# A hybrid state-space and delta-rule block: the modulation's shift leaves h and comes back as a bias per projection column

## The chip, the cores and the metric

The kernel runs on one NeuronCore of a Trainium2 chip. Its engines work side by side, each in the order of its own queue: TensorE (PE, matmuls; PEld is its loading of weights), VectorE (DVE), ScalarE (ACT), GpSimd (POOL), and SyncE (SP), which here only issues DMAs. SBUF is the working memory; PSUM holds what PE writes, in eight banks. The metric is the time of one execution in microseconds of device time, as the median of several runs.

## What is computed

The reference is one layer of an encoder block over 2048 tokens of 1024 features. The change touches its beginning only:

```python
mod = jax.nn.silu(c) @ ada_w + ada_b
shift, scale, gate = jnp.split(mod, 3, axis=-1)
h = rms_norm(x, norm_w) * (1.0 + scale[:, None, :]) + shift[:, None, :]
proj = h @ w_in            # 1024 x 3088
u_a, z_a, qkv, z_b, beta_fb, alpha_fb = jnp.split(proj, [o1, o2, o3, o4, o5], axis=-1)
...
y = jax.nn.gelu(y.reshape(bsz, seq, D_SSM)).astype(dt)          # S5 group, from u_a
qkv = jax.nn.silu(centred_depthwise_conv(qkv, conv_w))          # DeltaNet group
...
mix = jnp.concatenate([y_a, y_b], axis=-1) @ w_out
return x + gate[:, None, :] * mix                               # then a final rms_norm
```

There is one sequence, so shift, scale and gate are one vector of 1024 each. The projection of h is linear: what the shift adds to a column of `proj` is the same for all tokens, the product of the shift with that column of `w_in`.

## The kernel before

**Projection.** h is held transposed, features on partitions, as two f16 tensors `hhi` and `hlo` (a value and what its rounding leaves), 8 slices of 128 features by 2048 tokens. A block of 128 columns of `w_in` is held the same way, as `wh` and `wl`. One product (`gemm`, lines 244 to 247) is 24 matmuls of 128 by 512 tokens: for each of 8 slices wh by hhi, wh by hlo, wl by hhi, all into one PSUM bank. The 2048 tokens are four blocks of 512 (`NB`). `order` (line 182) lists 25 blocks of columns: 4 for u (the S5 input), then 3 z blocks, the 16 columns of beta and alpha (`ab`), and 17 further blocks of k, q, v and z.

**Scales.** Values are scaled by a power of two before they are rounded to f16, so that they fit. For weights, `w_max` takes a sum of squares on ACT (Square, line 203) and a ones-matmul on PE that spreads it over the partitions (line 208), and `w_cut` makes the scale on DVE (`pow2_root`), rounds `wh` on ACT (line 221) and makes `wl` on DVE (line 223). The inverse scale `iv` is multiplied by `ih`, the inverse scale of h (line 219). For h, `h_scale` takes a bound of the scale vector, and of the shift where there is one, over all features (a reduction on DVE and one on POOL).

**The opening stage** (lines 250 to 500) is written in the order in which each engine is to take its work (`manual_schedule`); every engine's queue follows the program's order. x arrives in blocks of 512 tokens; `x_square` (ACT), `x_root` and `x_scale` normalise it, `h_turn` transposes it on PE into PSUM, and `h_part` makes hhi and hlo. The modulation's columns are weighted sums of rows of `ada_w` (`aw_add` on DVE, the last two on POOL), summed over partitions by matmuls with a vector of ones (`mod_sum`, into the bank `pmod`). The scale's sum is made first, the shift's sum later.
- Block 0 is made twice. First without a shift and with a scale of its own, `s_0` (lines 377 to 380), so that the four products of u can run before the shift is known (lines 395 to 419, kept in four banks as `first`); at the end of the stage again with the final scale (lines 479 to 481).
- When the shift is known (lines 418 to 429), the final scale is set, `h_part` makes blocks 1 to 3 with the shift inside, in three steps: ACT writes scale times x plus shift in f32 (`hf`, line 318), POOL rounds it (line 320), DVE takes the difference (line 321).
- For block 0 of u alone, the shift comes as a bias: lines 435 to 439 multiply the u weights by the shift (one column, 24 matmuls a block of columns), and lines 453 and 454 empty the four kept banks with that bias. `u_out` (line 447) empties a bank with ACT and stores it to `u_d`.
- Then u of blocks 1 to 3, with `h_part` of the next block between the products. Beside them go loads and sums for the gate (`aw_add`, line 486), and in the last block `w_max` and `w_cut` of the first weights of the jobs (lines 495 to 500).

**The jobs** (`job`, line 984): for each of the other 21 blocks of columns, four products, each emptied by ACT into `raw` (line 1017, `conv_job`), `z` (line 1003, `z_job`) or `ab` (line 1116, `ab_job`); after the first product the next block's weights are loaded and squared, and later cut. After each product a `tick` (line 976) runs what is due of the convolutions, sums and transposes, and one step of the S5 group (`side`). PSUM has three tags: "gm" with two banks for products, "pt" with three and "sq" with three (line 85).

Of the kernel before, what the change touches and what calls it, by code (L numbers as in the profile page):

```python
# [23 lines left out]
KT = D // 128  # L24
# [16 lines left out]
def block(ctx, tc, x, c, ada_w, ada_b, norm_w, w_in, conv_w,  # L41
# [131 lines left out]
    ih = hpool.tile([128, 1], F32, name="ih")  # L173
    cw = s5t.tile([128, 12, 5], F32, name="cw")
# [20 lines left out]
    def w_max(i):  # L195
# [5 lines left out]
        m, ma, s, iv = [sp.tile([128, 1], F32, tag=f"w{j}", name=f"w{j}", bufs=6) for j in range(4)]  # L201
        wh, wl = [pools["wp", i < NU].tile([128, KT, order[i][1]], F16, tag=t, name=t) for t in ("wh", "wl")]
        A.activation(out=wl.bitcast(BF16), in_=ws, func=AF.Square, accum_out=m)
        wprep[i] = [None, ma, s, iv, wh, wl]
# [6 lines left out]
    def w_cut(i):  # L211

        if i >= len(order):
            return
        ps, ma, s, iv, wh, wl = wprep[i]
        ws = wraw[i]
        pow2_root(ps, ma, s, iv)
        if i >= NU:
            V.tensor_tensor(out=iv, in0=iv, in1=ih, op=ALU.mult)
        yield  # L220
        A.activation(out=wh, in_=ws, func=AF.Copy, scale=s)  # L221
        yield
        V.scalar_tensor_tensor(out=wl, in0=ws, scalar=s, in1=wh, op0=ALU.mult, op1=ALU.subtract)  # L223
        wprep[i] = (wh, wl, iv)
# [5 lines left out]
    def w_done(i):  # L230
        w = wprep[i][0:3]
        if i < NU:
            V.tensor_tensor(out=w[2], in0=w[2], in1=ih, op=ALU.mult)
        return w
# [15 lines left out]
    with ExitStack() as p0:  # L250
# [65 lines left out]
        def h_part(b, k, src):  # L316
            hf = hp.tile([128, 512], F32, tag="hf", name="hf", bufs=4)
            A.activation(out=hf, in_=src, func=AF.Identity, scale=aS[:, k:k + 1], bias=shS[:, k:k + 1])  # L318
            sl = slice(b * 512, (b + 1) * 512)
            P.tensor_scalar(out=hhi[:, k, sl], in0=hf, scalar1=1.0, scalar2=1.0, op0=ALU.mult, op1=ALU.mult)  # L320
            V.tensor_tensor(out=hlo[:, k, sl], in0=hf, in1=hhi[:, k, sl], op=ALU.subtract)
# [49 lines left out]
        s_0, ih0, s_h = [small(n) for n in ("s_0", "ih0", "s_h")]  # L371
        h_scale(bd, s_0, ih0, "h0")
        aS0, aS, shS = [small(n, KT) for n in ("aS0", "aS", "shS")]
        V.tensor_scalar(out=aS0, in0=aT, scalar1=s_0, scalar2=None, op0=ALU.mult)
        cuts = {i: w_cut(i) for i in range(1, NU)}

        for k in range(KT):
            A.activation(out=hhi[:, k, 0:512], in_=xk[:, k], func=AF.Copy, scale=aS0[:, k:k + 1])
            V.scalar_tensor_tensor(out=hlo[:, k, 0:512], in0=xk[:, k], scalar=aS0[:, k:k + 1], in1=hhi[:, k, 0:512],
                                   op0=ALU.mult, op1=ALU.subtract)  # L380
# [4 lines left out]
        ss = x_square(x1)  # L385
        first = []
        iv0 = small("iv0", NU)
# [7 lines left out]
        first.append(gemm(wprep[0], 0))  # L395
        next(cuts[2])
        next(cuts[2])
        shift_add(0, 1)
        whole(cuts[2])
        first.append(gemm(wprep[1], 0))  # L400
        whole(w_max(3))
# [3 lines left out]
        next(cuts[3])  # L405
        next(cuts[3])
        shift_add(2, 3)
        whole(cuts[3])
# [5 lines left out]
        first.append(gemm(wprep[2], 0, "sq"))  # L414
        turned = [h_turn(x1, k, t) for k, t in enumerate(("pt", "pt", "sq"))]
        first.append(bank("sq"))
        gemm_part(first[3], wprep[3], 0, range(4))
        mod_sum(0, [acc, aws[6]])
        gemm_part(first[3], wprep[3], 0, range(4, KT))
        xs_ = {2: x_load(2)}  # L420
        V.tensor_tensor(out=modc[:, 0:8], in0=pmod[:, 0:8], in1=adab[:, 0:8], op=ALU.add)
        V.scalar_tensor_tensor(out=bs_, in0=modc[:, 0:8], scalar=-1.0, in1=modc[:, 0:8], op0=ALU.mult, op1=ALU.max)
        V.tensor_tensor(out=bd, in0=bd, in1=bs_, op=ALU.add)
        h_scale(bd, s_h, ih, "h")
        V.tensor_scalar(out=aS, in0=aT, scalar1=s_h, scalar2=None, op0=ALU.mult)
        V.tensor_scalar(out=shS, in0=modc[:, 0:8], scalar1=s_h, scalar2=None, op0=ALU.mult)
        sh = [hp.tile([128, KT], F16, name=n, bufs=1) for n in ("shh", "shl")]
        V.tensor_copy(out=sh[0], in_=shS)
        V.tensor_tensor(out=sh[1], in0=shS, in1=sh[0], op=ALU.subtract)
        for k in range(3):  # L430
            h_part(1, k, turned[k])
# [1431 lines left out]
```

## Time and profile before

| | us |
|---|---|
| median of 3 runs | 1407.08 |
| lowest and highest | 1400.67, 1408.08 |
| the profiled execution | 1399.43 |
| its span, first to last instruction | 1397.7 |
| PE busy in the span | 1282.3 |
| DVE busy | 1017.6 |
| POOL busy | 708.1 |
| ACT busy | 672.5 |
| first u product starts | 40.18 |
| first product of block 1 starts | 85.74 |
| first product of the jobs starts | 165.82 |
| last z eviction of the jobs starts | 766.8 |

All rows but the first two come from one execution, taken by the hardware profiler. Times in its views count from the start of the span. A busy PE is modelled from the starts of its matmuls. The chain of waits goes back from the last instruction, at each step to what released it; the list of an engine's waits names the instruction that ended each wait last.

### The profile page before, as it was taken

What the parts mean: (1) busy time and instruction counts of PE and PEld (TensorE: products, weight loads), DVE (VectorE), ACT (ScalarE), POOL (GpSimd) and SP (SyncE); (2) the same over time, 40 slices, a digit from 0 to 9 for tenths busy, and PEclk for the clock granted to TensorE, in tenths of its full rate; (3) what the DMA queues carried; (4) which work ended last, traced back from release to release, by engine and by line L of the source; (5) the groups of instructions that cost most, each with busy time, mean ns of one, the idle gap of its engine ahead of it and who ended that gap; (6) DMA issues with size and microseconds to landing.
All of it is one profiled execution on the core that took longest, in us unless ns stands there. A gap on an engine that the chain in (4) does not pass through costs nothing.

```text
span 1397.7 us, 26524 instructions
## 1 busy us (share of the span) xinstructions
PE 1282.3 (92%) x9936; PEld 900.3 (64%) x9936; DVE 1017.6 (73%) x2095; ACT 672.5 (48%) x1348; POOL 708.1 (51%) x680
## 2 busy tenths in 40 slices
PE   2879897898999999999999699999999988998997
PEld 2445343355665555555554588999998877887885
DVE  4635579877765899998984667888878655865664
ACT  4445322444655454354445566776667423432332
POOL 3214223656540477878840766666553235654443
PEclk9789999999999999999999899999999999999998
DMA  9446343223457434343524533544335488686533
GB/s 308 173 86 187 92 87 87 64 82 89 121 163 191 132 106 129 99 143 95 156 80 135 163 83 96 175 144 143 115 132 184 150 294 279 223 312 211 181 107 112
DMA packets 255280, 206.43 MB, mean 148 GB/s; under 512 B 88496, under 2 KB 206256, under 8 KB 255152
## 3 DMA queue, kind: packets, MB, share of 16 engines
q1 hardware_dynamic: 255152, 204.75, 47.3%
q8 instruction: 78, 1.28, 0.4%
q14 instruction: 50, 0.41, 0.1%
HBM read 133.38 MB, written 73.33 MB: 148 GB/s over the span
## 4 chain that ended last, share of the span: by engine, by line
PE 67%; DVE 16%; DMA 4%; issue 3%; POOL 3%; ACT 2%; SPq 1%; DVEq 0%; POOLq 0%; ACTq 0%
PE gm L33 37%; PE sq L33 15%; PE pt L33 12%; DVE sq L1033 2%; DVE w L510 2%; DVE tm L510 1%; DVE xs L939 1%; PE pt L1077 1%; POOL w L510 1%; DMA y<-ya_d 1%; DVE t L510 1%; PE sq L1750 1%; DMA xt<-in_x_dram 0%; DVE r L1782 0%; DVE cv L1033 0%
## 5 line engine op out<-in xcount | busy, mean ns | idle before, releaser
L33 PE MATMUL gm<-hhi,wh 128*128 128x512 f16 (+1 forms) x784 | 294.4, 390 | 13.4 <-ACT wh L221 6.9
L33 PE MATMUL gm<-hhi,wl 128*128 128x512 f16 (+1 forms) x784 | 293.1, 388 | 8.2 <-DVE wl L223 8.2
L33 PE MATMUL gm<-hlo,wh 128*128 128x512 f16 (+1 forms) x784 | 293.4, 389 | 0.0
L33 PEld LDWEIGHTS <-wh 128*128 128x128 f16 (+1 forms) x1664 | 154.0, 100 | 199.7 <-issue 26.0
L33 PEld LDWEIGHTS <-wl 128*128 128x128 f16 (+1 forms) x832 | 79.8, 100 | 106.1 <-DVE wl L223 10.7
L1017 ACT ACTIVATE raw<-gm,w 128x512 f32<-128x512 f32 x48 | 33.1, 689 | 175.9 <-PE gm L33 175.9
L510 POOL TENSOR_TENSOR w<-w,w 128x512 f32<-128x512 f32 x32 | 50.2, 1578 | 87.9 <-DVE w L510 87.9
L33 PE MATMUL gm<-yh,gwh 128*128 128x256 f32 x256 | 80.0, 313 | 6.7 <-ACT yh L778 5.6
L1033 DVE SCALAR_TENSOR_TENSOR sq<-raw,cw,cv 128x512 f32<-128x512 f32 x48 | 55.2, 1151 | 29.6 <-ACT cv L1025 29.5
L1033 DVE SCALAR_TENSOR_TENSOR sq<-raw,cw,sq 128x512 f32<-128x512 f32 x96 | 72.6, 756 | 3.4
L33 PE MATMUL gm<-yl,gwh 128*128 128x256 f32 x256 | 73.3, 286 | 0.7 <-POOL yl L779 0.7
L1772 POOL TENSOR_TENSOR r<-r,xt 128x512 f32<-128x512 f32 x32 | 41.5, 1297 | 62.9 <-DVE r L1771 29.2
L33 PE MATMUL gm<-yh,gwl 128*128 128x256 f32 x256 | 72.5, 283 | 0.0
L1442 ACT ACTIVATE Y<-pt 128x512 f16<-128x512 f32 x96 | 58.0, 604 | 23.9 <-PE pt L33 23.2
L33 PE MATMUL sq<-S,kq 128*128 128x128 f32 x480 | 62.3, 281 | 0.0
L939 DVE TENSOR_TENSOR_SCAN xs<-c,w 128x255 f32<-128x255 f32 x64 | 61.1, 1013 | 1.1 <-POOL w L510 1.1
L33 PEld LDWEIGHTS sq<-S,kq 128*128 128x128 f32 x480 | 59.9, 196 | 2.0
L1421 DVE CAST_PREDICATED pb<-msk,pt 128x512 f16<-128x512 int8 x80 | 56.9, 714 | 5.5 <-PE pt L33 4.4
L1003 ACT ACTIVATE z<-gm,w 128x512 f32<-128x512 f32 x32 | 22.0, 688 | 80.0 <-PE gm L33 48.0
L33 PE MATMUL pt<-Y,nh 128*128 128x64 f16 (+1 forms) x896 | 56.3, 198 | 4.5 <-DVE Y L1429 4.2
L320 POOL TENSOR_SCALAR hhi<-hf 128x512 f16<-128x512 f32 x32 | 30.1, 960 | 54.9 <-ACT hf L318 47.9
L1443 ACT ACTIVATE YT<-pt 128x512 f16<-128x512 f32 x96 | 57.3, 597 | 0.0
(455 smaller groups left out, 3544.9 us busy)
## 6 DMA issues: line engine op xcount, KB each, us to landing
xt<-in_x_dram SPq DMA_DIRECT2D x25, 512.0 KB
ws<-in_w_in_dram SPq DMA_DIRECT2D x24, 512.0 KB
aw<-in_ada_w_dram SPq DMA_DIRECT2D x24, 512.0 KB
kq<-kT_d SPq DMA_DIRECT2D x32, 256.0 KB
kq<-qT_d SPq DMA_DIRECT2D x32, 256.0 KB
kt<-kt_d SPq DMA_DIRECT2D x32, 256.0 KB
vt<-vt_d SPq DMA_DIRECT2D x32, 256.0 KB
out_dram<-r SPq DMA_DIRECT2D x16, 512.0 KB
```

Of the source, the lines that this page charges most:

```text
L33: nc.tensor.matmul(out, lhsT, rhs, start=start, stop=stop)
L320: P.tensor_scalar(out=hhi[:, k, sl], in0=hf, scalar1=1.0, scalar2=1.0, op0=ALU.mult, op1=ALU.mult)
L510: (e or V).tensor_tensor(out=o, in0=a, in1=b, op=op)
L939: V.tensor_tensor_scan(out=o, data0=m1, data1=v, initial=0.0, op0=ALU.mult, op1=ALU.add)
L1003: A.activation(out=z, in_=ps, func=AF.Silu, scale=iv)
L1017: A.activation(out=raw[:, 2 + tb * 512:2 + (tb + 1) * 512], in_=ps, func=AF.Copy, scale=iv)
L1033: V.scalar_tensor_tensor(out=cv if j == 4 else ps, in0=raw[:, o + j:o + j + 512], scalar=cw[:, i12, j:j + 1], in1=cv if j == 1 else ps, op ...
L1077: nc.tensor.transpose(ps[:, j * 128:(j + 1) * 128], cv[:, j * 128:(j + 1) * 128], ident)
L1421: V.copy_predicated(out=cols(PB[d][li], b, d), mask=mb, data=pp.rearrange("p t (n b) -> p t n b", b=b))
L1442: A.activation(out=cols(Y[d], b, d), in_=pa.rearrange("p t (n b) -> p t n b", b=b), func=AF.Copy)
L1443: A.activation(out=cols(YT[d], b, 1 - d), in_=pb.rearrange("p t (n b) -> p t n b", b=b), func=AF.Copy)
L1772: P.tensor_tensor(out=r[:, ns], in0=r[:, ns], in1=xt[:, ns], op=ALU.add)
```

## The change

The shift is taken out of h and is added behind each product, as a bias per column.
- `h_part` has no shift and two steps: ACT rounds scale times x to `hhi`, DVE makes `hlo` from the same source, the PSUM bank. POOL has no part in it. It serves block 0 too, which is made once, with one scale of h (`s_h`, `ih`) that is known before the shift.
- The shift gets a scale of its own (`s_s`, inverse `ish`) and stays in SBUF as two f16 columns per slice, `sh`.
- A new function `w_bias` multiplies one block of weights by the shift: 24 matmuls of one column into a "pt" bank, and a copy on ACT with the scale `ib`, which is the weights' inverse scale times `ish` (one more multiplication on DVE for each block of weights). It is called for the four u blocks in the opening stage, and at the start of every job ahead of its first product; for the beta and alpha columns it runs 96 matmuls, since their weights stand at four places.
- Evictions of the products take the bias with them (Identity and Silu with a bias in place of Copy and Silu).
- In the opening stage the u products of block 0 and the first two of block 1 are emptied without a bias, into the slots of `xk` that block 0 has left (`u_raw`); when the biases are there, POOL adds them and the stores go out (`u_add`). Block 1 is rounded between the products of block 0. The weight cut of the third u block is put ahead of the squares of block 1, the squares of the fourth ahead of the scaling of x, the squares, root and scaling of block 2 ahead of the shift's scale.
- The second making of block 0 at the end of the stage is gone.

The diff, without the parts that only carry the new value along:

```diff
@@ w_max / w_cut
-        m, ma, s, iv = [sp.tile([128, 1], F32, tag=f"w{j}", name=f"w{j}", bufs=6) for j in range(4)]
+        m, ma, s, iv, ib = [sp.tile([128, 1], F32, tag=f"w{j}", name=f"w{j}", bufs=6) for j in range(5)]
...
         if i >= NU:
+            V.tensor_tensor(out=ib, in0=iv, in1=ish, op=ALU.mult)
             V.tensor_tensor(out=iv, in0=iv, in1=ih, op=ALU.mult)
...
+    def w_bias(w, n, rows=(0,)):
+
+        ps = bank("pt")
+        for k in range(KT):
+            for a, b, j in ((0, 0, 0), (0, 1, 1), (1, 0, 2)):
+                for r in rows:
+                    mm(nc, ps[r:r + n, 0:1], w[a][:, k, :], sh[b][:, k:k + 1], k + j == 0, k == KT - 1 and j == 2)
+        wb = sp.tile([128, 1], F32, tag="wb", name="wb", bufs=NU)
+        for r in rows:
+            A.activation(out=wb[r:r + n], in_=ps[r:r + n, 0:1], func=AF.Copy, scale=w[3][r:r + n])
+        return wb
...
         def h_part(b, k, src):
-            hf = hp.tile([128, 512], F32, tag="hf", name="hf", bufs=4)
-            A.activation(out=hf, in_=src, func=AF.Identity, scale=aS[:, k:k + 1], bias=shS[:, k:k + 1])
             sl = slice(b * 512, (b + 1) * 512)
-            P.tensor_scalar(out=hhi[:, k, sl], in0=hf, scalar1=1.0, scalar2=1.0, op0=ALU.mult, op1=ALU.mult)
-            V.tensor_tensor(out=hlo[:, k, sl], in0=hf, in1=hhi[:, k, sl], op=ALU.subtract)
+            A.activation(out=hhi[:, k, sl], in_=src, func=AF.Copy, scale=aS[:, k:k + 1])
+            V.scalar_tensor_tensor(out=hlo[:, k, sl], in0=src, scalar=aS[:, k:k + 1], in1=hhi[:, k, sl],
+                                   op0=ALU.mult, op1=ALU.subtract)
...
+        def u_add(b, ct):
+            ur = raws.pop((b, ct))
+            P.tensor_scalar(out=ur, in0=ur, scalar1=ub[ct], scalar2=1.0, op0=ALU.add, op1=ALU.mult)
+            u_store(b, ct, ur)
...
+        whole(cuts[2])
+        ss = x_square(x1)
+        u_raw(0, 0)
+        mx = w_max(3)
+        next(mx)
         rs = x_root(ss)
         for j in range(4):
             x_scale(x1, rs, j, (A, P)[j % 2])
-        next(cuts[3])
-        next(cuts[3])
+        u_raw(0, 1)
+        whole(mx)
+        whole(cuts[3])
+        turns = ("pt", "sq")
+        u_raw(0, 2)
+        shift_add(0, 1)
+        for k in range(0, 4):
+            h_part(1, k, h_turn(x1, k, turns[k % 2]))
         shift_add(2, 3)
-        whole(cuts[3])
+        u_raw(0, 3)
+        for k in range(4, KT):
+            h_part(1, k, h_turn(x1, k, turns[k % 2]))
+        xs_ = {2: x_load(2)}
         shift_add(4, 5)
...
+        u_raw(1, 0)
+        ss = x_square(xs_[2])
         mod_sum(0, [acc, aws[6]])
+        rs = x_root(ss)
+        for j in range(4):
+            x_scale(xs_[2], rs, j, V)
         V.tensor_tensor(out=modc[:, 0:8], in0=pmod[:, 0:8], in1=adab[:, 0:8], op=ALU.add)
...
+        u_raw(1, 1)
+        ub = []
         for ct in range(NU):
+            ib = wprep[ct][3]
+            V.tensor_tensor(out=ib, in0=ib, in1=ish, op=ALU.mult)
+            ub.append(w_bias(wprep[ct], 128))
+        for b, ct in ((0, 0), (0, 1), (0, 2), (0, 3), (1, 0), (1, 1)):
+            u_add(b, ct)
...
-                elif ct < 2:
-                    for k in range(4 * ct, 4 * ct + 4):
-                        h_part(0, k, xk[:, k])
...
     def job(i, evac):
-        w = w_done(i)
+        w = wprep[i]
+        wb = w_bias(w, 128)
         for tb in range(NB):
             ps = gemm(w, tb)
-            evac(tb, ps, w[2])
+            evac(tb, ps, w[2], wb)
...
     def ab_job(i):
-        wh, wl, iv = w_done(i)
+        wh, wl, iv = wprep[i][0:3]
+        wb = w_bias(wprep[i], 16, [32 * j for j in range(NB)])
         ps = bank("gm")
```

More of the change, by code (lines that the diff above doesn't have):

```diff
@@ L370, in block @@
         V.tensor_scalar(out=bd, in0=bd, scalar1=float(D) ** 0.5, scalar2=None, op0=ALU.mult)
[L371 to L374, printed above, removed]
+        s_h, s_s = small("s_h"), small("s_s")
+        h_scale(bd, s_h, ih, "h")
+        aS, shS = small("aS", KT), small("shS", KT)
+        V.tensor_scalar(out=aS, in0=aT, scalar1=s_h, scalar2=None, op0=ALU.mult)
         cuts = {i: w_cut(i) for i in range(1, NU)}
         for k in range(KT):
-            A.activation(out=hhi[:, k, 0:512], in_=xk[:, k], func=AF.Copy, scale=aS0[:, k:k + 1])
-            V.scalar_tensor_tensor(out=hlo[:, k, 0:512], in0=xk[:, k], scalar=aS0[:, k:k + 1], in1=hhi[:, k, 0:512],
-                                   op0=ALU.mult, op1=ALU.subtract)
+            h_part(0, k, xk[:, k])
             if k in (1, 3, 5):
@@ L384, in block @@
                 whole(w_max(2))
-        ss = x_square(x1)
-        first = []
-        iv0 = small("iv0", NU)
+        raws = {}
         def shift_add(*ks):
@@ L421, in block @@
         V.tensor_tensor(out=modc[:, 0:8], in0=pmod[:, 0:8], in1=adab[:, 0:8], op=ALU.add)
         V.scalar_tensor_tensor(out=bs_, in0=modc[:, 0:8], scalar=-1.0, in1=modc[:, 0:8], op0=ALU.mult, op1=ALU.max)
[L423 to L427, printed above, removed]
+        h_scale(bs_, s_s, ish, "s")
@@ L440, in block @@
-        for k in range(3, KT):
-            h_part(1, k, h_turn(x1, k, ("sq", "pt")[k % 2]))
-        ub = small("ub", NU)
-        for ct in range(NU):
-            V.tensor_scalar(out=ub[:, ct:ct + 1], in0=pmod[:, 16 + ct:17 + ct], scalar1=uw[ct][2], scalar2=None,
-                            op0=ALU.mult)
-        def u_out(b, ct, ps, iv, **kw):
-            ur = up.tile([128, T, 64], F32, tag="u", name="u")
-            A.activation(out=ur, in_=ps.rearrange("p (r t) -> p t r", t=T),
-                         func=AF.Identity if kw else AF.Copy, scale=iv, **kw)
-            nc.sync.dma_start(out=u_d[ct * 128:(ct + 1) * 128, :, b * 64:(b + 1) * 64], in_=ur)
@@ L453, in block @@
-        for ct in range(NU):
-            u_out(0, ct, first[ct], iv0[:, ct:ct + 1], bias=ub[:, ct:ct + 1])
+            ib = wprep[ct][3]
[3 more added lines that the diff above has]
+            u_add(b, ct)
         pada.close()
```

76 lines of the change are left out of this document (36 added, 40 removed).

## The prediction

> **What bounds the kernel now.** I read the page first, then PE's waits and the chain of waits in the opening stage (the rows from 40 to 172 us, which hold nearly all that the change reorders), then the same chain for the projection jobs, where the change adds work.
>
> ```profile
> span 1397.7 us, 26524 instructions
> ...
> PE 67%; DVE 16%; DMA 4%; issue 3%; POOL 3%; ACT 2%; SPq 1%; DVEq 0%; POOLq 0%; ACTq 0%
> ...
> L33 PEld LDWEIGHTS <-wh 128*128 128x128 f16 (+1 forms) x1664 | 154.0, 100 | 199.7 <-issue 26.0
> ```
>
> PE has two thirds of the chain that ended last. So work added to PE's queue is paid for wherever PE leads, and a wait taken out of PE's queue is a gain. The profiled execution took 1399.43 us (its span of 1397.7 and 1.7 around it); that is 7.65 below the median of 1407.08, so I add my sum to the median and not to the span. What can be told from no change here is 0.5%, or 7.0 us.
>
> PE's waits from 40 to 172 us (total, times, longest):
>
> ```profile
> PE pt L33 <- ACT wl L203: 12.2, 2, 7.6
> PE gm L33 <- ACT u L449: 6.5, 1, 6.5
> PE sq L313 <- ACT hf L318: 1.8, 1, 1.8
> ```
>
> The 7.6 in the first row lies before the first u product and stays. The chain of waits shows where the others come from (start, length, what):
>
> ```profile
> 63.21 4.21 PE pt L33 x32
> ...
> 69.82 2.13 ACT hf L318 x3
> ...
> 75.50 0.62 POOL hhi L320
> ...
> 85.74 17.90 PE gm L33 x72
> ```
>
> Read it as one string: the shift is summed on PE (63.21), and only then can h of block 1 be made, ACT to POOL to DVE, and only then are the banks of block 0's four products emptied (the ACT u L449 of the waits above); block 1's products start at 85.74. The same stage ends with a second hole, and with it I quote where the jobs begin:
>
> ```profile
> 151.72 0.59 PE L33 MATMUL pt<-w,ones 128*128 128x1 f32 x2 [4.63 <-ACT wl L203]
> ```
>
> ```profile
> 165.82 5.20 PE gm L33 x24
> ```
>
> The clock is part of the price. In the table of stretches (length, then busy time of PE, PEld, DVE, ACT and POOL) the number after POOL's is the granted clock:
>
> ```profile
> 66.30:69.70 3.40, 3.40 (x12) 1.83 (x12) 1.50 (x10) 0.00 (x0) 0.41 (x1) 0.50 0.00 0
> 69.70:73.10 3.40, 3.40 (x34) 1.66 (x33) 0.36 (x3) 2.12 (x3) 0.00 (x0) 0.50 0.02 7
> ...
> 86.70:90.20 3.50, 3.50 (x10) 1.23 (x9) 0.00 (x0) 0.99 (x2) 0.00 (x0) 0.50 0.82 196
> ...
> 151.60:155.10 3.50, 3.38 (x10) 1.47 (x11) 3.50 (x5) 0.07 (x1) 2.17 (x2) 0.51 0.84 228
> ```
>
> Half clock stands after the shift's sum, after the 6.5 us wait and after the 4.6 us wait; products run there at half speed.
>
> **The change, part by part.** *Opening stage, what goes.* With the shift out of h, block 1's h no longer waits for it: the waits of 6.5 and 1.8 go (8.3 us). The second hole came from the last eight `h_part`s (block 0 made a second time with the final scale), which stood on ACT ahead of the Square of the first job's weights. They are gone. What is left between the end of the product and PE's ones-product is an eviction and a Square with its read:
>
> ```profile
> L294 ACT ACTIVATE jk<-xt 128x1024 bf16<-128x1024 f32 x12 | 12.6, 1054 | 0.3
> ...
> L449 ACT ACTIVATE u<-gm,w 128x512 f32<-128x512 f32 x12 | 8.2, 687 | 41.5 <-PE gm L33 41.5
> ...
> L203 ACT ACTIVATE wl<-ws 128x1024 bf16<-128x1024 f32 x3 | 3.1, 1041 | 0.0
> ```
>
> 0.69 + 1.04 and about 0.2 make 1.9, so 4.6 becomes 1.9: 2.7 us. The half clock goes with the holes: of 66.3 to 72.3, about 5 us were products (half lost, 2.5); of 85.74 to 90.2, 4.4 (2.2); of 152.3 to 155.1, 2.8 (1.4): 6.1 us. Two waits of 0.2 go as well. Together 8.3 + 2.7 + 6.1 + 0.4 = 17.5 us.
>
> *Opening stage, what comes.* DVE now has roundings of block 1 (`h_part`, from PSUM) between the shift's additions, so the additions end later, and with them the 32-matmul sum, which sits in PE's queue ahead of the product (1, 1) and the biases.
>
> ```profile
> L279 DVE SCALAR_TENSOR_TENSOR acc<-aw,sc,acc 128x1024 f32<-128x1024 f32 x5 | 7.2, 1439 | 0.1
> L379 DVE SCALAR_TENSOR_TENSOR hlo<-xk,aS,hhi 128x512 f16<-128x512 f32 x8 | 5.7, 747 | 2.2 <-ACT hhi L378 2.2
> ```
>
> Additions 7.2 + 0.7 and eight roundings 5.7 (taken for a PSUM source as for this SBUF one) are 13.6 us of DVE after the last weight cut, which my schedule places near 57.4 (an estimate); with 0.6 of small operations the sum can start between 71.6 and, if POOL's own adds slow DVE further, 74.9. PE gets there near 73: the old sum at 63.21 stood after three and a half products; half a product more, one whole (5.2 each, from the row at 165.82) and five transposes, some 2.2, make 10. I take 2.0 us of wait. The sum still brings the half clock: products run on until a full stretch has passed, about 4.3 us at half speed, 2.1 lost. Together with 0.3 for small order effects, 4.4 us. The squares, root and scaling of block 2 (4 x 1.05 on ACT, then DVE) now stand before the shift's scale on DVE; by my schedule the scaled shift is there at 86, as the product (1, 1) ends at 86.4, so I cost that at nothing; if that product were warm, PE would wait 2 us. On SP's queue six u stores, the gate and conv loads come before block 3's load: I find it landed near 110 us, where its squares need its first rows at 108.5 and the last at 112, so nothing again; it would cost 1 to 3 if the stores were later. `hhi` leaves POOL, which now only adds the bias to six stored blocks, off the path. Net of the opening stage: 17.5 - 4.4 = 13.1 us gained, the bounds 9 (the sum's half clock lasting twice as long, and the wait on the scaled shift) and 16 (no wait for the sum).
>
> *Jobs, what comes.* Every one of 20 jobs now begins with 24 one-column matmuls on PE, before its first product. The same 96 instructions stand in the old kernel for the u columns:
>
> ```profile
> 72.34:74.84 2.50, 2.50 (x97) 2.50 (x96) 0.00 (x0) 0.00 (x0) 0.00 (x0) 0.84 0.02 7
> ```
>
> 2.50 us for 96, 26 ns each, 24 are 0.625 us per job. Whether that is paid for depends on who leads there. The chain by line, from 166 to 767 us:
>
> ```profile
> by line: PE gm L33 47.0%; PE sq L33 9.4%; DVE sq L1033 5.1%; DVE w L510 3.7%; PE pt L33 3.1%; DVE tm L510 2.8%; DVE xs L939 2.8%; issue 2.6%; PE pt L1077 2.1%; POOL w L510 2.1%; DVE t L510 1.7%; DVE cv L1033 1.0%; POOL rt L510 1.0%; DVE cu
> ```
>
> PE has 61.6 of the 84.4 points that are listed, 73%; so 14 of 20 biases are on the path, 8.75 us; the others meet a wait of PE for DVE and vanish in it. The weights' load is inside the 26 ns. The Trainium skill, "TensorE: Matmul & The Clock Gate", section "LDWEIGHTS (loading the stationary operand)", gives a load as columns over 1.2 GHz, 107 ns for 128 columns; by that rule a job's 24 would take 2.6 us, 14 jobs 28 us more than in my sum, and the median would be near 1434. The row above contradicts it for this form (26 ns, load and product together), and I keep the row.
>
> The job of the beta and alpha columns adds 96 matmuls of 16 columns (four rows each). Its gemm stood partly in the shadow of a wait, and narrow matmuls in different column groups follow each other faster than 26 ns:
>
> ```profile
> 240.79 0.61 PE L33 MATMUL gm<-hhi,wl 128*16 128x512 f16 x4 [2.19 <-DVE wl L223]
> ...
> 247.43 0.50 PE L33 MATMUL sq<-cpw,bbr 64*32 64x128 f32 x13
> ```
>
> I take 1.2 us (12 ns each; bound 2.5 at 26 ns) and 1.0 for the eight products that ran before the 2.19 us wait and now come after it: 2.2 us, all on the path.
>
> DVE gets one more 128x1 multiplication per weight block, of the form of L219:
>
> ```profile
> L219 DVE TENSOR_TENSOR w<-w,ih x21: 115/787/1136, 158.4 to 739.8; 128x1 f32<-128x1 f32 x21
> ```
>
> 115 ns when nothing is in the way, 787 in the median. It comes right behind its twin, so I take 0.3 and count it where DVE leads, 6 jobs: 1.8 us (bounds 0.7 and 4.7). Evictions with a bias, a small eviction of the bias itself and the u stores are on engines that do not lead; the evictions' 0.09 (0.78 against 0.69) I cost at nothing. Jobs in all: 8.75 + 2.2 + 1.8 = 12.75 us lost, bounds 8 and 17.
>
> **Sum.** 13.1 gained, 12.75 lost: -0.35 us. So the profiled time would be 1399.1, and the median 1407.08 - 0.35 = 1406.7.
>
> **The rivals.** *The jobs hide the additions.* If PE's products in the jobs have slack that the profile does not show (a busy PE there is modelled), only the biases up to the first conv jobs and the beta-alpha job are paid, about 5 us, and the opening stage gains all of 13 to 16: 8 to 11 us faster, 1397.5. Against it: after 340 us PE's visible waits are few.
>
> ```profile
> PE sq L33 <- DVE cv L1033: 2.0, 2, 1.2
> PE sq L33 <- DVE w L510: 1.9, 2, 1.2
> ```
>
> They can take in 3.9 us and no more. For it: the bounds of both sums (16 and 8) reach that far with no new mechanism.
>
> *PE waits for a bank at the start of a job (the slower side).* The bias takes one of three "pt" banks directly behind a tick's transposes and sums, whose banks are read a tick later by DVE or at once by ACT.
>
> ```profile
> L1096 ACT ACTIVATE kk<-pt x16: 570/576/581, 352.2 to 459.6; 128x512 f32<-128x512 f32 x16
> ```
>
> If PE must wait for that copy behind an eviction (0.58 + 0.69 = 1.27 us) at the 11 conv job starts from K1 to V3, that is 14 us: 1420.7. It decides from 0.67 us a start. Against it: each job already takes a pt bank for the weights' sum, without a wait of PE on ACT among its waits after 340 us; but that comes five microseconds after the tick, the bias at once.
>
> *The opening gain halves.* The scaled shift comes late (behind block 2's squares, root and scaling on DVE), the half clock returns twice, block 3's load holds up its squares: 13.1 falls to about 5.3, and the whole loses 7.5: 1414.6.
>
> *The weight loads are not hidden.* At the 100 ns of the page's row of loads, 24 cost 2.4 us and not 0.625: 14 x 1.8 = 25 us slower, 1432. This is the mechanism behind the cited rule; the row of 96 in 2.50 us speaks plainly against it.
>
> **How the numbers follow.** Forecast (within 0.5%) 0.53; hidden additions 0.27, faster; bank wait 0.12, halved opening 0.06, unhidden loads 0.02, slower. Faster 0.27, same 0.53, slower 0.20. The range reaches from 1395 (below the hidden case, whose bounds give 16 - 5 = 11 us) to 1416 (above the halved opening) and leaves out the bank wait, the loads and the far end of the hidden case, some 0.18.
>
> **What would show it.** In the changed profile: the first product of block 1 follows block 0's without a hole, near 67 us instead of 85.74; the first job's first matmul near 153 (165.82 - 13.1), with under 2 us of wait before the ones-product of its weights; 24 one-column matmuls in about 0.63 us ahead of each job, and the last job ending about where it ended before. It is wrong if jobs start with a PE wait on ACT (the bank), if the one-column matmuls are 60 ns or more apart, if PE waits for the scaled shift, or if the job phase grew by under 8 or over 17 us.

## The result, and the profile after

The changed kernel takes 1412.69 us (median of 6 runs, 1409.96 to 1417.05), the kernel before 1405.53 beside it (6 runs): a ratio of 1.006, with an interval of 1.0039 to 1.008. In a second session of 6 runs the ratio was 1.0058 (1.0036 to 1.0081). The change makes the kernel slower by about 8 us. The forecast was 0.35 us faster.

Two profiles of each kernel give the ledger. "First z eviction" is the start of ACT's first eviction in the jobs; "jobs" goes from there to the start of the last one; the "tail" is the rest of the span, where the two kernels have the same instructions.

| us | first z eviction | jobs | tail | span |
|---|---|---|---|---|
| before | 171.04, 172.82 | 595.8, 596.9 | 630.9, 631.8 | 1397.7, 1401.5 |
| after | 162.46, 164.24 | 613.7, 612.7 | 636.6, 634.3 | 1412.7, 1411.2 |
| mean of after less mean of before | -8.6 | +16.8 | +4.1 | +12.4 |

The opening stage gave back less than the 13.1 us forecast, and the jobs lost more than the 12.75. First the opening stage: PE's waits from 40 to 172 us in the profile after (total, times, longest).

```profile
PE pt L33 <- ACT wl L206: 2.0, 1, 2.0
PE pt L33 <- DVE shh L463: 1.9, 1, 1.9
PE pt L323 <- DVE xt L317: 1.3, 4, 0.3
```

The waits of 6.5 and 1.8 us on ACT's u and hf are gone, as forecast, and the ones-product's wait is 2.0 instead of 4.6. (The wait ahead of the first u product, 7.4 us here, ends at 39.5 and so falls out of this window.) The second and third rows are new: the first bias waits for the scaled shift, and PE's transposes of block 3 wait for DVE's scaling of x. The end of the stage in the chain of waits (start, length, what):

```profile
142.80 12.07 PE gm L33 x48
154.87 2.30 PE pt L33 x28
157.17 5.22 PE gm L33 x24
```

The first job's product starts at 157.17 (165.82 before, in the same view). The 48 matmuls in the first row would take 10.36 at the full clock, as they do in several runs below. The stretches from 143.50 on (length, then busy time of PE, PEld, DVE, ACT and POOL, and the granted clock) show why they took 12.07, and show the same thing once more in the jobs:

```profile
143.50:146.90 3.40, 3.40 (x9) 1.18 (x8) 1.29 (x9) 0.00 (x0) 0.00 (x0) 0.51 0.65 175
...
433.70:437.10 3.40, 3.40 (x10) 1.21 (x9) 1.75 (x8) 0.00 (x0) 0.00 (x0) 0.50 0.61 143
```

A clock of 0.5, for 3.4 us, with PE busy from end to end. The second stretch has no counterpart in the kernel before. What stands in front of it is in PE's rows by time (start, duration, instruction, idle time before it and its releaser):

```profile
430.10 0.95 PE L33 MATMUL pt<-ones,sq 128*128 128x1 f32 x8
432.15 0.16 PE L33 MATMUL pt<-shh,wh 128*128 128x1 f16 x1 [1.10 <-ACT kk L1114]
...
432.73 0.16 PE L33 MATMUL pt<-shh,wl 128*128 128x1 f16 x1
432.76 0.38 PE L33 MATMUL gm<-hhi,wh 128*128 128x512 f16 x1
```

This is the start of job Q2. The bias takes a "pt" bank, and the bank is still being copied out by ACT (the kk copy), so PE stands for 1.10 us; 24 matmuls in 0.61 us follow, and 0.9 us later the clock is halved. Some of PE's waits from 290 to 790 us (the largest, 5.1 us on ACT's yh, is 5.6 in the kernel before and is left out):

```profile
PE pt L33 <- ACT kk L1114: 2.8, 3, 1.5
PE sq L33 <- DVE w L527: 2.6, 3, 1.2
PE pt L1095 <- DVE kss L1083: 2.5, 1, 2.5
PE sq L33 <- DVE cv L1051: 1.8, 2, 0.9
```

The first of these rows is the wait for a bank that the second rival named: at 3 starts of a job, not at 11.

### The profile page after: what moved, and what is told of

It reads as the page before. It is cut to its first block, busy times and chain, and to the rows that moved or that the text cites. A ratio compares the mean times of both kernels' runs of the same rounds, so it can differ in the third digit from the quotient of the medians.

```text
span 1412.7 us, 27672 instructions
## 1 busy us (share of the span) xinstructions
PE 1302.0 (92%) x10512; PEld 918.0 (65%) x10512; DVE 1008.1 (71%) x2106; ACT 678.2 (48%) x1368; POOL 680.0 (48%) x654
## 4 chain that ended last, share of the span: by engine, by line
PE 68%; DVE 14%; DMA 2%; issue 2%; ACT 2%; POOL 1%; SPq 1%; DVEq 0%; ACTq 0%; POOLq 0%
PE gm L33 37%; PE sq L33 16%; PE pt L33 13%; DVE sq L1051 2%; DVE w L527 1%; DVE xs L956 1%; PE pt L1095 1%; DMA of<-o_d 1%; DMA kq<-qT_d 1%; DVE tm L527 1%; DVE pb L1440 1%; DVE YT L1453 1%; PE sq L1769 1%; DVE t L527 0%; DVE cv L1051 0%
## 5 line engine op out<-in xcount | busy, mean ns | idle before, releaser
L33 PE MATMUL gm<-hhi,wh 128*128 128x512 f16 (+1 forms) x800 | 301.6, 393 | 0.0
L33 PE MATMUL gm<-hlo,wh 128*128 128x512 f16 (+1 forms) x800 | 301.1, 392 | 0.0
L33 PE MATMUL gm<-hhi,wl 128*128 128x512 f16 (+1 forms) x800 | 301.1, 391 | 0.0
L33 PEld LDWEIGHTS <-wh 128*128 128x128 f16 (+1 forms) x2048 | 167.5, 100 | 197.0 <-issue 31.3
L33 PEld LDWEIGHTS <-wl 128*128 128x128 f16 (+1 forms) x1024 | 93.1, 99 | 107.5 <-DVE wl L227 11.4
L1035 ACT ACTIVATE raw<-gm,wb,w 128x512 f32<-128x512 f32 x48 | 37.4, 779 | 176.2 <-PE gm L33 176.2
L1021 ACT ACTIVATE z<-gm,wb,w 128x512 f32<-128x512 f32 x32 | 24.9, 778 | 70.7 <-PE gm L33 44.0
L227 DVE SCALAR_TENSOR_TENSOR wl<-ws,w,wh 128x1024 f16<-128x1024 f32 (+1 forms) x25 | 32.6, 1306 | 34.0 <-ACT wh L225 33.9
```

The source lines that it names most:

```text
L33: nc.tensor.matmul(out, lhsT, rhs, start=start, stop=stop)
L1021: A.activation(out=z, in_=ps, func=AF.Silu, scale=iv, bias=wb)
L1035: A.activation(out=raw[:, 2 + tb * 512:2 + (tb + 1) * 512], in_=ps, func=AF.Identity, scale=iv, bias=wb)
```

## The experiments

All ratios are to the kernel before, run beside each of them; 0.001 is 1.4 us. The differences between two such ratios are uncertain by some 0.003, so where an edit moves the time by less than 5 us its place in the profile carries the argument. Each run in the table has one profile.

| run | ratio (interval) | first z eviction | jobs | tail |
|---|---|---|---|---|
| changed kernel, again | 1.0058 (1.0036 to 1.0081) | 164.2 | 612.7 | 634.3 |
| no bias in the jobs | 0.9955 (0.9936 to 0.9973) | 164.4 | 597.4 | 635.9 |
| bias made twice | 1.0222 (1.0196 to 1.0249) | 165.8 | 631.0 | 638.1 |
| bias behind the first product | 1.0004 (0.9988 to 1.002) | 162.4 | 605.6 | 634.5 |
| bias in another bank | 1.0032 (1.0018 to 1.0045) | 161.2 | 610.3 | 635.8 |
| no beta-alpha bias | 1.0054 (1.0034 to 1.0073) | 164.3 | 611.5 | 635.4 |
| six additions on DVE | 1.0027 (1.0007 to 1.0047) | 161.3 | 612.2 | 635.7 |
| block 3 loaded first | 1.0016 (1.0002 to 1.003) | 159.1 | 613.6 | 636.3 |
| squares one product earlier | 1.0015 (1.0 to 1.003) | 159.3 | 611.5 | 633.6 |
| all moves | 0.9977 (0.9963 to 0.9991) | 157.7 | 608.9 | 634.5 |
| best | 0.9932 (0.9909 to 0.9956) | 159.2 | 602.0 | 634.8 |
| best, two columns | 0.9922 (0.99 to 0.9943) | 157.4 | 600.5 | 637.2 |

### What the biases of the jobs cost

The first run replaces every bias of the jobs by a column of zeros; the biased evictions and DVE's extra multiplication stay.

```diff
-        wb = w_bias(w, 128)
+        wb = zb0
...
-        wb = w_bias(wprep[i], 16, [32 * j for j in range(NB)])
+        wb = zb0
```

> The changed kernel without the bias of the jobs: a column of zeros stands for it, so the shift is left out of z, q, k, v, beta and alpha; the evictions and the extra multiplication on DVE stay. Theory A (the loss sits in the jobs, in the one-column matmuls on PE, the bank waits and the half clock behind them): the job phase shrinks by 15 of its 17.7 us, about 1398 us, ratio to before 0.994. Theory B (the loss sits in DVE's extra multiplication and in the evictions with a bias, which stay here): only 3 to 5 us come back, ratio 1.002.

The time fell by 0.0105, 14.8 us, and the jobs are 15.8 us shorter than the mean of the two changed profiles. They come within 0.5 to 1.7 us of the jobs before, so the evictions with a bias and DVE's multiplication together cost no more than that; the theory that they carry the loss falls. The loss of the jobs comes with the bias products. The opposite edit makes each bias twice:

```diff
+        w_bias(w, 128)
         wb = w_bias(w, 128)
```

> The bias of each of the 20 full jobs is computed twice in a row (the first result unused). Theory A, that each set of 24 one-column matmuls costs its 0.63 us wherever PE leads: 15 x 0.63 = 9.5 us more than the changed kernel, ratio to before about 1.013. Rival C, that a set costs only because PE must wait for a bank: the second set finds its bank free or waits for the first, 2 to 4 us more, ratio 1.008; if the set vanishes in waits, nothing.

It cost 0.0162, about 23 us: more than the 20 times 0.61 us of matmuls that were added, so both expectations were too low. PE's waits of this run, from 290 to 800 us, say what came with them:

```profile
PE pt L33 <- DVE iq L1080: 6.9, 3, 3.7
PE pt L33 <- ACT kk L1115: 2.7, 3, 1.5
PE pt L33 <- ACT wb L243: 2.0, 4, 0.9
```

Two biases in a row take two of the three "pt" banks: PE now waits on DVE's read of sums (iq, 6.9 us) and on the first bias's own eviction (wb). New half-clock stretches follow such waits too. This one comes behind 1.48 us of waiting on kk and 0.88 us on wb:

```profile
374.20:377.60 3.40, 3.25 (x31) 1.59 (x31) 3.09 (x12) 0.36 (x2) 0.00 (x0) 0.50 0.90 249
```

In the last 7 jobs (from z3's last eviction to the end of the jobs) none of these waits stands, and there the second bias cost 4.2 us, 0.60 a job: its matmuls alone. So the price of a bias has two parts, its matmuls and its place. The next run moves it behind the first product of its job; its bank is asked for 5 us later, and it is still made before the first eviction.

```diff
-        wb = w_bias(w, 128)
         for tb in range(NB):
             ps = gemm(w, tb)
+            if tb == 0:
+                wb = w_bias(w, 128)
```

> The bias of each full job is computed behind its first product instead of ahead of it; nothing else changes. Theory A: the 0.63 us stay, but the waits for a pt bank (2.8 us in sum) and the half clock that follows the long run of narrow work at a job start (434 to 437 us, 546 to 550 us) go: 4 to 6 us faster than the changed kernel, ratio to before 1.001 to 1.002. Rival C (bank waits are most of the loss): 10 us or more faster. If the waits only move: no difference.

It won 0.0056, 7.9 us, and the jobs are 7.6 shorter. The wait on kk is not among PE's waits from 290 to 790 us any more. The rows on DVE's cv, kss and w are now

```profile
PE sq L33 <- DVE cv L1052: 1.9, 2, 1.0
PE pt L1096 <- DVE kss L1084: 1.5, 1, 1.5
PE sq L33 <- DVE w L527: 1.4, 2, 0.8
```

and around the same start of a job the clock stays whole (the changed kernel first, then this run):

```profile
420.00:445.00 25.00, 23.74 (x148) 13.52 (x147) 13.28 (x27) 11.40 (x19) 0.78 (x2) 0.93 0.69 168
```

```profile
415.00:440.00 25.00, 24.83 (x163) 14.49 (x162) 15.05 (x30) 11.40 (x19) 2.15 (x4) 1.00 0.71 167
```

In the same 25 us PE gets through 15 more instructions. One profile each could be chance, so look at the others: of the six that keep one bias at the head of a job in a "pt" bank, five have a half-clock stretch that begins between 430 and 436 us, and none of the other profiles has one. Over all the jobs the gain in clock is small: 30.7 us at half clock in both profiles of the changed kernel, 27.3 here, since a stretch at 521.1 is new. That is worth 1.7 us; with the 2.8 us of the bank and 2.0 us at the first K job (below) it makes 6.5 of the 7.6. The 8.2 us of jobs that remain between this run and the one without biases are what the matmuls themselves cost: two thirds of the 12.2 us by which PE is busy longer. Is it the bank, or the place at the head of the job? The bias at its old place, in a bank of the other kind:

```diff
-        ps = bank("pt")
+        ps = bank(tag)
...
-        wb = w_bias(w, 128)
+        wb = w_bias(w, 128, tag="sq")
```

> The bias of each job stands where it stood, ahead of the first product, but takes a bank of the kind sq instead of pt. Theory E (what a job's start loses over 0.6 us is the wait for a pt bank that ACT copies out, with the half clock behind it): the wait of PE on ACT's kk copy is gone (2.8 us, 3 times) and so are the half-clock stretches at 433.7 and 546.3, 4 to 6 us less as with the bias behind the first product, ratio 1.0015 to 1.003. Rival F (24 one-column products at the start of a job cost by their place, whatever bank they take): no difference, ratio 1.006. Rival G (the sq banks are held by DVE's convolutions, about 2.5 us each): PE waits on DVE instead, ratio 1.006 to 1.012.

0.0028 won, 3.9 us, with 2.9 in the jobs; that is about the uncertainty. From 290 to 790 us the wait on kk is gone, and so are the half-clock stretches at 433.7 and 546.3 (one at 493 is new, behind a wait of 2.22 us on cv), but the "sq" banks have waits of their own (the first row is the one left out above):

```profile
PE gm L33 <- ACT yh L795: 5.1, 2, 4.4
PE sq L33 <- DVE cv L1051: 4.6, 4, 2.2
PE pt L1095 <- DVE kss L1083: 2.5, 1, 2.5
```

The wait on DVE's convolutions (cv) grew from 1.8 to 4.6. So the wait on kk is one for the kind of bank, as theory E says, and rival G's wait comes in its stead at a smaller price; that place alone costs nothing is not shown.

### The beta-alpha job

```diff
-        wb = w_bias(wprep[i], 16, [32 * j for j in range(NB)])
+        wb = sp.tile([128, 1], F32, tag="wbz", name="wbz")
+        V.memset(wb, 0.0)
```

> The beta-alpha job alone has a column of zeros in place of its bias (its 96 narrow matmuls and four small evictions are left out; beta and alpha lack the shift); all 20 other biases stay. Theory I (in this job the whole product stands behind the bias, which needs both rounded halves of the weights, so the eight products that used to run under the wait now come after it, in half clock): last eviction of K0 minus last eviction of z2 falls from 41.7 us to near 38, 3.5 to 4.5 us less in the time, ratio near 1.003. Rival J (the forecast's price of 2.2 us): 39.5, ratio 1.0045. Rival K (the job's length is set by DVE's table work, and by how early PE gets there): no difference, 41.7, ratio 1.006.

Theory I falls: the ratio moved by 0.0004 to 0.0006 only. The theory had read z2's last eviction, which ACT makes late in this place; PE's own rows are the better measure. From the end of z2's last product to the first product of K0 the two traces before have 18.6 and 19.4 us, the changed ones 22.8 and 22.0, this run 21.8, and the run without any job bias 19.2. So the 96 narrow matmuls cost 0.2 to 1.0 us. K0's bias behind them shows in the stretch from the end of the beta-alpha products to K0's first product: 4.0 us in the changed kernel's two profiles and in this run's, 1.9 in the two traces before, in the run without job biases and in the one with the bias behind the first product. So K0's bias costs 2.0. The changed kernel's rows show why K0's is the dear one:

```profile
243.54 0.18 PE L33 MATMUL pt<-shh,wh 128*128 128x1 f16 x1 [0.90 <-ACT wh L225]
245.01 0.18 PE L33 MATMUL pt<-shh,wl 128*128 128x1 f16 x1 [1.27 <-DVE wl L227]
```

The weights have only just been cut. Without a bias, two 512-column matmuls of the product run while DVE makes wl; with it, two matmuls of 26 ns do, and PE stands for the rest.

### The opening stage

Between block 2's first product (103.54 in the changed kernel) and the first job's product the time is nearly what it was, 53.5 us (53.4 before), though a wait of 2.6 us is gone from it. The queue of POOL and then that of SP in the changed kernel:

```profile
82.95 0.41 POOL L338 PARTITION_ALL_REDUCE sma<-sm  x1 [14.23 <-DVE sm L337]
90.60 4.02 POOL L409 TENSOR_SCALAR xk<-xk,wb 128x512 f32<-128x512 f32 x6 [7.24 <-issue]
```

```profile
91.31 5.76 SPq L413 DMA_DIRECT2D u_d<-xk  x6
97.12 1.14 SPq L478 DMA_DIRECT2D gate<-in_ada_b_dram  x1
98.31 7.00 SPq L480 DMA_DIRECT2D cw<-in_conv_w_dram  x5
105.42 3.75 SPq L296 DMA_DIRECT2D xt<-in_x_dram  x4
```

The first bias had left ACT at 85.7, but POOL took up its additions at 90.60, 7.24 us after the reduction over partitions and waiting for nothing that the profile shows ("issue"). The stores wait for them, and block 3's load stands behind the stores. Two edits free the load from this wait. One gives the six additions to DVE:

```diff
-            P.tensor_scalar(out=ur, in0=ur, scalar1=ub[ct], scalar2=1.0, op0=ALU.add, op1=ALU.mult)
+            V.tensor_scalar(out=ur, in0=ur, scalar1=ub[ct], scalar2=1.0, op0=ALU.add, op1=ALU.mult)
```

> The bias of the first six u blocks is added on DVE instead of POOL. In the changed kernel POOL starts these 7.2 us after its reduction over partitions, though the bias is there 5 us earlier, and the stores, the gate and conv loads and block 3's load on SP stand behind. Theory A: block 3 lands some 4 us earlier, PE's wait for its transposes (1.3 us of waits, 2.2 us with the slower transposes) goes: 2 us faster than the changed kernel, ratio 1.005. Rival: block 3's load is set by the conv loads' own queue and nothing moves: no difference.

The other puts the load ahead:

```diff
+        xs_[3] = x_load(3)
         for b, ct in ((0, 0), (0, 1), (0, 2), (0, 3), (1, 0), (1, 1)):
             u_add(b, ct)
...
-                        xs_[3] = x_load(3)
                         w_dma(NU)
```

> Block 3's load is issued ahead of the six u stores instead of behind them, the gate and the conv weights. Theory C (the opening stage lost 2 of its forecast 13.1 us because the stores waited for POOL's bias additions, which began at 90.60, and block 3's load stood behind them on SP until 105.42): the load goes out near 86, PE's transposes of block 3 follow each other without the wait of 1.6 us at 119.56, and the third product of block 2 loses its 0.5: first z eviction near 160.4 (162.46 in the changed kernel), time 2 us below the changed kernel, ratio to the kernel before near 1.0045. Rival: the wait at 119.56 is DVE's own lateness (x scaling in its queue) and not the load's: no difference, ratio 1.006.

They won 0.0033 and 0.0044 (4.6 and 6.2 us). In both, block 2's first product and the first job's lie 49.75 us apart and not 53.5, and the wait of PE's transposes on xt is gone. The second run's only wait of PE from 82 to 165 us, and SP's loads in it (block 2's four and block 3's four are one group):

```profile
PE pt L33 <- ACT wl L206: 2.0, 1, 2.0
```

```profile
60.71 8.06 SPq L296 DMA_DIRECT2D xt<-in_x_dram  x8
91.67 0.63 SPq L413 DMA_DIRECT2D u_d<-xk  x1
```

So, against this profile, the late load cost 2.0 us in the transposes and the product before them, and the half clock behind the ones-product, 1.7, went with it, although the hole of 2.0 us before the ones-product stayed. The third edit takes that hole and leaves the late load:

```diff
+                if b == NB - 1 and ct == 0:
+                    mx = w_max(NU)
+                    next(mx)
                 if b == NB - 1 and ct in (1, 2):
                     if ct == 1:
-                        whole(w_max(NU))
+                        whole(mx)
```

> The Square of the first job's weights stands on ACT one product earlier (behind block 3's first u eviction), so PE's ones-product finds it done. Theory D (the hole of 1.9 us at 142 costs itself and the half clock of 143.5 to 146.9 behind it): 1.9 + 1.7 = 3.6 us less, first z eviction near 158.9, ratio near 1.0035. Rival: the half clock follows the narrow products and the earlier waits (transposes of block 3 at 119.56), not this hole, so it comes all the same: 1.9 us less, first z eviction 160.6, ratio 1.0047.

0.0045 won, 6.3 us, 4.0 of it (53.5 to 49.5) between the same two products: the hole and the half clock behind it, as theory D had it. But a hole of 2.0 us brought that half clock in the changed kernel and did not in the two runs before this one. Their stretches ahead of it, with the same PE time, don't differ in any column that would tell why (the changed kernel, then the additions on DVE; both end where a stretch of 3.41 us, counted on from the half-clock stretches of the same run, ends):

```profile
140.09:143.50 3.41, 1.46 (x8) 0.63 (x7) 1.94 (x2) 1.81 (x3) 0.00 (x0) 1.00 0.75 259
```

```profile
139.43:142.84 3.41, 1.46 (x7) 0.49 (x5) 0.81 (x1) 1.81 (x3) 0.00 (x0) 1.00 0.75 290
```

Nor is it the edits alone. Seven profiles have this part of the program unedited: the two of the changed kernel and those of the five runs on the jobs' biases. Between 100 and 160 us half clock stands behind the ones-product in two of them (at 143.5, and at 145.1 in the run without the beta-alpha bias), earlier in four, among the transposes of block 3 and the product behind them (from 121.6 to 123.7 us on), and nowhere in one, with the bias in another bank, though both waits are there (1.0 and 2.0 us). In the second profile of the changed kernel it stands at 123.7, and the time between the two products is 54.1; in the run with the other bank it is 51.3. In all six profiles with the load or the hole edited there is none. So an edit takes the half clock away, but which hole it follows changes between executions of the same program, and the split into 2.0 and 1.7 us holds for the first profile only. What decides stays open.

### Together

All of these edits, with the additions on DVE and the beta-alpha job's bias behind its gemm:

```diff
+            if tb == 0:
+                wb = w_bias(w, 128)
...
+            V.tensor_scalar(out=ur, in0=ur, scalar1=ub[ct], scalar2=1.0, op0=ALU.add, op1=ALU.mult)
...
+        xs_[3] = x_load(3)
...
+                    next(mx)
...
+        wb = w_bias(wprep[i], 16, [32 * j for j in range(NB)])
         w_dma(i + 2)
```

> Everything together: bias behind the first product of a job (measured -6.1 against the changed kernel), bias of the six stored blocks added on DVE (-4.6) with block 3's load ahead of the stores, squares of the first job's weights one product earlier, and the beta-alpha job's bias behind its gemm. Theories A to E as a sum: -6.1 -4.6 -1.9 (the hole, its half clock being in the 4.6 already) -0.5 = -13 against the changed kernel, 1400, ratio near 0.9955. Rival H (half clock returns at other places as soon as a hole goes, so gains don't add): -8, ratio near 0.9995.

0.9977: 11.7 us won of the 13 that the sum gave. It beats the kernel before. One of the moves was a loss: with the beta-alpha bias behind its products, ACT takes the four small evictions ahead of the Square of K0's weights, PE waits 2.4 us for that Square, and the stretch from z2's last product to K0's first is 22.7 us, against 20.0 in the run that moved only the bias of the other jobs. The next leaves the additions on POOL and the beta-alpha bias in front, and instead squares and cuts K0's weights ahead of the beta-alpha gemm:

```diff
         wh, wl, iv = wprep[i][0:3]
+        w_dma(i + 2)
+        whole(w_max(i + 1))
+        whole(w_cut(i + 1))
         wb = w_bias(wprep[i], 16, [32 * j for j in range(NB)])
```

> Bias behind the first product of a job, block 3's load ahead of the stores, the squares of the first job's weights one product earlier, and in the beta-alpha job the next job's weights are squared and cut ahead of the gemm and not behind it. Theories A to E and I: from the run with all moves (0.9977) the last edit takes the stretch from the end of the gemm to K0's first product (4.05 us in the changed kernel) down to about 1: -3 us, ratio near 0.9955. Rival H (half clock comes back somewhere else, or DVE's table work sets the pace there): 0.9975.

0.9932, about 9.5 us under the kernel before and 18 under the changed one; the jobs are 602.0. PE now waits at one place for both blocks of weights, and 0.7 us lie between the end of the beta-alpha products and K0's first product, instead of 4.0:

```profile
227.50 0.58 PE L33 MATMUL pt<-w,ones 128*128 128x1 f32 x2 [6.42 <-ACT wl L206]
229.90 0.18 PE L33 MATMUL pt<-shh,wl 128*16 128x1 f16 x4 [1.68 <-DVE wl L227]
```

This edit and the earlier squares would serve the kernel before as well; they were not tried there, so the 9.5 us are not the worth of the change. Last, the bias in 16 matmuls:

```diff
-            for a, b, j in ((0, 0, 0), (0, 1, 1), (1, 0, 2)):
+            for a in ((0, 1) if k < KT - 1 else (1, 0)):
...
+                    mm(nc, ps[r:r + n, 0:2 - a], w[a][:, k, :], shc[:, k, 0:2 - a], k + a == 0, k == KT - 1 and a == 0)
...
+            A.activation(out=w2[r:r + n], in_=ps[r:r + n, 0:2], func=AF.Copy, scale=w[3][r:r + n], accum_out=wb[r:r + n])
```

> The kernel of the run before it, with both halves of the shift as two columns of one operand: 16 matmuls per bias (8 of two columns, 8 of one) and not 24, the two sums added by the eviction. Theory A (a one-column matmul with its load costs 26 ns, one of two columns hardly more): 8 x 26 ns = 0.2 us less per bias, of 25 biases (a u column each counted, too) some 16 on the path: -3.3 us, ratio 0.0024 below that of the run before it. Rival: a bias's price is its fixed part (bank, waits): no difference.

0.001 less, within the uncertainty; the jobs are 1.5 us shorter. Their place settles more than the time: from z3's last eviction to the last one, 7 jobs, this run takes 211.65 us, and ten profiles with 24 matmuls for each bias take 213.00 to 213.13. That is 0.2 us a job, as theory A has it.

### The base, and the tail

> The changed kernel once more, with nothing edited, so that the other runs have a base of more than six executions. Every theory: ratio 1.006, inside 1.004 to 1.008. If it comes out at 1.004 or less, the gains of the single edits are that much smaller than told so far.

> The kernel before, once more and with nothing edited, for a second profile of it. Theory L (the 5.7 us by which the changed kernel's tail, from the last eviction of the jobs to the end, is longer in the two profiles come from a short profiled run of the kernel before, and not from the change): a tail of 634 to 637 us, jobs again near 595.8, span near 1402 to 1404. Rival M (the tail is longer because the jobs end at another phase of the clock): a tail of 631 again, span near 1398.

The changed kernel came out as before (1.0058). The kernel before, again, has a ratio to itself of 0.9999 (0.9983 to 1.0016), its tail is 631.8 and its span 1401.5. The tail is rival M's and speaks against L; M's mechanism is not shown by that. Every profile of a kernel with the change or a part of it has a tail of 633.6 to 638.1. The same instructions run there, so this is not work. The clock differs in places, as from 1077 to 1093 us, here in the second profile of the kernel before and the first of the changed one:

```profile
1077.00:1093.00 16.00, 13.86 (x195) 13.04 (x194) 14.70 (x27) 11.33 (x22) 0.61 (x1) 1.00 0.69 235
```

```profile
1077.00:1093.00 16.00, 13.79 (x161) 13.21 (x160) 14.74 (x28) 9.26 (x15) 2.15 (x2) 0.89 0.76 261
```

A mean of 0.89 is one half-clock stretch, worth at most 1.7 of the 4 us, and other places make up for it: over the whole tail the granted clock is 0.96 in both profiles before, and 0.97 and 0.96 after. PE is busy there for 584.8 and 584.9 us before, 587.7 and 586.9 after, so some 2.5 of the 4.1 us may come from half clock that falls on denser work; as a busy PE is modelled, this is not shown. The cause of the longer tail stays open. The profiled executions of the kernel before were also 3.6 and 6.1 us under the medians beside them, and those of the changed kernel 1.3 us under and 1.7 over, so part of the ledger's 12.4 us against the 8 of the medians lies in which executions were profiled.

## Why the prediction was wrong, point by point

By the profiles the forecast was 12.7 us short: 4.5 in the opening stage (8.6 gained and not 13.1), 4.1 in the jobs (16.8 lost and not 12.75), and 4.1 in the tail, which the forecast had as unchanged. By the medians it was some 8 us short.

**The gain of the holes: right.** Block 2's first product starts at 103.54 and 104.76 in the two profiles, 112.25 and 112.58 before: 8.3 us earlier on the mean, where the forecast's terms up to there (13.1 less the 2.7 and 1.4 of the second hole) make 9.0. Block 1's first product starts at 66.5 (67 forecast). The sum of the shift was late by 0.3 us in the first profile and 1.9 in the second (2.0 forecast). The scaled shift was late by 1.9 in the first and not in the second, where the forecast had nothing, or 2 us if the product before it were warm.

**The load of block 3: the step that failed in the opening stage.** "On SP's queue six u stores, the gate and conv loads come before block 3's load: I find it landed near 110 us ... so nothing again; it would cost 1 to 3 if the stores were later." The stores were later, by POOL's pause, and it cost 2.0 us in the first profile (in the seven profiles without an edit here PE's waits on xt are 1.0 to 3.6 us). The pause stood in the trace of before as well, behind the reduction of the old kernel:

```profile
75.50 5.42 POOL L320 TENSOR_SCALAR hhi<-hf 128x512 f16<-128x512 f32 x7 [6.74 <-issue]
```

The prediction quoted the chain's 0.62 us of this instruction, and not the idle time ahead of it. Putting the bias additions behind the other reduction put such a pause onto the path of a load.

**The second hole: the hole right, its clock wrong.** 4.6 became 2.0, as 2.7 us of gain said. "The half clock goes with the holes" did not hold here: in the first profile it stayed, with 1.7 us, and it was gone in every run that took away the late load or the hole. Up to the first job's product the gain is 8.6 us (157.17 against 165.82, and as much between the second profiles), or 9.2 with the 0.6 us of the first job's bias, which the prediction had put under the jobs. That is at the lower bound of 9.

**The jobs: the matmuls right, their place the step that failed.** The 26 ns a matmul and 0.61 us a bias came as forecast, and where PE leads a bias is paid in full: from z3's last eviction to the end, 7 jobs, the distance to the kernel before grows by 4.0 us, 0.57 a job. The Trainium skill, "TensorE: Matmul & The Clock Gate", section "Wait — 56ns, not 53.3ns?", states about 25 ns from start to start as the least for any number of columns; the rows of the jobs' biases agree (24 in 0.61 us). "14 of 20 biases are on the path" fits as well: of the 12.2 us by which PE is busy longer with the biases behind the first product, 8.2 were paid, with the beta-alpha job in it, less than the 10.95 that the prediction had for both. The step that failed is that it took the place at the head of a job for free. That place cost 7.6 to 7.9 us more: the wait for a bank, the weights of K0 that had just been cut, and the half clock. The two errors go against each other, so the jobs came out only 4.1 us off the forecast.

**The bank wait: the rival that came, in a smaller form.** It was priced at 1.27 us times 11 starts, with "0.67 us a start" as the point from which it decides, and set at nothing in the forecast. It came at 3 starts, 2.8 us together and 1.5 at most, and two half-clock stretches (433.7, 546.3) were gone when the bias moved, with a new one at 521.1. For the first its place behind the wait is shown, and five of six profiles repeat it; the second, in four of the six, also had other waits ahead of it, and no row singles out its cause. A wait and a later reduction of the clock were priced in the opening stage, yet the jobs' price knew the wait alone.

**DVE's multiplication: in size right. The beta-alpha job: cheaper, and K0 dearer.** 0.5 to 1.7 us against 1.8, together with the evictions; 0.2 to 1.0 for the beta-alpha bias against 2.2, with 2.0 instead of 0.6 for the bias behind it. **Evictions of 0.78 instead of 0.69**: no cost found, as forecast. **The tail** was taken to be unchanged; it was 4 us longer in the profiles, and the cause is open.

## What to carry to other kernels

Price an added piece of work by its place as well as its length: which buffer it asks for at that moment and who still holds it, and what the short stop does to the clock afterwards; a few us later in the same queue it may cost half, or more, as in the beta-alpha job, if it then stands ahead of something that PE will wait for. When an operation moves behind another on an engine, look at the idle time that the old trace shows behind that other operation, "issue" too, and follow every DMA that stands behind its result. A gain worked out for one hole and its clock is only had if no neighbouring hole of the same size appears, and where the half clock stands is read from several executions, not from one.

## What the runs showed of the hardware

POOL took up no work for 6.74 and 7.24 us after a reduction over partitions of 0.41 us, in the trace before and in the one after, without a wait that the profile shows. Half clock came behind holes of PE of only 1.1 us (ahead of 433.7) and 2.0 us (ahead of 143.5), and stays for 3.4 us or a multiple; a hole of 2.0 us did not always bring it. It came without a hole as well: from 71.90 to 75.30 us of the changed kernel PE was busy for 3.32 of 3.40 us with the one-column matmuls of the shift's sum, and from 75.3 to 78.7 the clock was 0.5. So the 24 one-column matmuls of a bias may have a part in the half clock at the head of a job; no run separates them from the wait. The Trainium skill, "TensorE: Matmul & The Clock Gate", section "What's actually happening", has a free-running stretch of 3413 ns, and the lengths agree (3.4, 6.8, 10.2); its section "HAM oscillation — how this bites in real kernels" gives as a rule that PE should have no idle gaps of more than about 3.4 us, and the rows here show that less than that can be enough.
